# Two tiles of scores in flight in both attentions, and inversion blocks of one request beside the diagonal of the other

## The chip, the cores and the metric

One core of a Trainium2 chip runs the whole kernel. The metric is the device time of one execution in microseconds (us): 2386.69 is the median of three runs (2381.04 to 2390.11). The engines are TensorE (PE, with its weight loads PEld), VectorE (DVE), ScalarE (ACT), GpSimd (POOL) and SyncE (SP, which here issues nearly all DMAs).

## The reference

One encoder layer for two requests of 2048 tokens with 1024 features and shared weights. One projection feeds four mixing groups; their gated outputs are concatenated and projected back.

```python
def encoder_layer(x, mem, ...):
    hx = rms_norm(x, pre_g)
    a_u, a_z, b_qkv, b_z, b_gates, c_qkv, c_z, d_q, d_z = jnp.split(hx @ w_in, IN_SPLITS, axis=-1)
    y_a = fourier_mix(a_u, w_fnet) * jax.nn.silu(a_z)
    y_b = gdn_branch(b_qkv, b_gates, conv_w, a_log, dt_bias, gdn_g) * jax.nn.silu(b_z)
    cq, ck, cv = (t.reshape(b, l, N_HEADS_G, HEAD_DIM) for t in jnp.split(c_qkv, 3, axis=-1))
    y_c = neighbourhood_attn(cq, ck, cv, rpb) * jax.nn.silu(c_z)
    y_d = memory_attn(d_q, rms_norm(mem, mem_g), w_mem_kv) * jax.nn.silu(d_z)
    out = jnp.concatenate([y_a, y_b, y_c, y_d], axis=-1) @ w_out
    return x + rms_norm(out, post_g)
```

The gated DeltaNet group (GDN, `gdn_branch`) solves, for each chunk of 64 tokens, a unit lower triangular system `eye + l_mat`, in both directions of time, and then carries a state from chunk to chunk. Neighbourhood attention (NA) lets each token of a 32 x 64 grid see a window of 8 rows by 16 columns. Memory attention lets each token see 256 memory tokens of its request.

## The kernel before

Every matrix product is done in split fp16: the high and low half of each operand, three matmuls (`mm3`, L502: high by high, high by low, low by high). The program is written stage by stage in `build` (L1692). Each stage runs under a priority (`band`, L202), and a scheduler merges the stages at build time into one list for each engine, which that engine works off in its order. So a line that is written earlier need not run earlier. Tiles are taken from pools: a tile with `bufs` of n is n buffers in turn, and the n+1st waits for the last reader of the first. Pools lie on two stacks, left and right, and a pool in memory that another has left waits for that one's last users, stores included. PSUM banks are shared by tag in the same way.

The stages, as they follow in time:

- The GEMM passes: `pj` tiles on PE, evacuated to `st` tiles, stored to DRAM. `pass_z` and `pass_b` go on as fillers beside all that follows, up to 2000 us.
- `gdn_sub` (L1027), on the right stack, once for each request r. Each 64 x 64 triangle is inverted as two diagonal blocks of 32 and one block between. The diagonal: 31 steps on POOL (tile `pr`) and on DVE (PSUM tile `ppr`, tag `as`), each a product (L1064) and a sum (L1066). Then the results are split in halves (ACT L1079 and L1087, DVE L1080 and L1088) and stored to DRAM as `T` and `TO` (L1081, L1082, L1089); the parts go through `ol`, `lo`, `A` and `pr`. The blocks between: four tiles a request (d = 0, 1 and q = 0, 1), each with loads `ob`, a copy to `lb`, products `px` (tag `ga` for q = 0, `as` for q = 1), a split to `zb`, products `pz`, a split to `z`, and stores to `T`. Before the change request 0 is done in full, pool `psub0` and then `pblk0`, and request 1 then opens `psub1`.
- The GDN chain (`gdn_chain`, L1194): 32 steps, products `pc` and `pw`, loads of `T` by `cT`.
- Memory attention (`mem_attn`, L1458), on the left stack: 32 tiles, scores `pms`, softmax, transpose by DMA `mPT`, values `pmo`, output `pmy`. Its `na_setup` builds NA's bias table.
- NA (`na_attn`, L1551): 64 tiles. `scores`: products `pns` on PE, bias and maximum on DVE (`nS`), exponential on ACT, split into one of four padded tiles `np` (ACT L1640, DVE L1641), and a DMA transpose to `nPT` (L1643, two buffers). `values`: products `pno` with the loaded `nv`, evacuated by ACT to `nya` (L1669), stored as `yc` (L1671). As the code is written, the scores of tile i + 1 stand ahead of the values of tile i.
- The output projection (`pass_o`, L680, products `po`), 365 us. Its pool opens when the left stack is free, after NA.

Of the kernel before, what the change touches and what calls it, by code (L numbers as in the profile page):

```python
# [8 lines left out]
F32 = mybir.dt.float32  # L9
# [143 lines left out]
class Kern:  # L153
# [873 lines left out]
    def gdn_sub(self, r, side):  # L1027


        nc, D = self.nc, self.D  # L1030
        H = (slice(0, 32), slice(32, 64))
        row = lambda t, sl: t[:, sl].unsqueeze(1).to_broadcast([P, 32, 32])
        with self.tc.tile_pool(name=f"psub{r}", bufs=1, side=side) as pp:
            tl = lambda shape, dt, nme, b=1: pp.tile(shape, dt, name=self.nm(nme), tag=nme, bufs=b)
            Lu, nb, be, lp, T = {}, {}, {}, {}, {}
            zero = tl([P, 64], F16, "zero")
            nc.gpsimd.memset(zero, 0.0)
            for d in range(2):
                Lu[d] = D[f"L{r}_{d}"].rearrange("n h (q s) c -> (n h q) s c", q=2)
                self.dt([P, 64, 2, 2, 32], F16, f"T{r}_{d}")  # L1040
                self.dt([P, 32, 3, 2, 32], F16, f"TO{r}_{d}")
                nb[d], be[d] = tl([P, 64], F32, f"nbu{d}"), tl([P, 64], F32, f"beu{d}")
                nc.sync.dma_start(nb[d], D[f"nbd{r}"][d].rearrange("n h (q c) -> (n h q) c", q=2))
                nc.sync.dma_start(be[d], D[f"bed{r}"][d].rearrange("n h (q c) -> (n h q) c", q=2))

                lp[d] = tl([P, 2, 32, 32], F32, f"A{d}")
                for b in range(2):
                    nc.sync.dma_start(lp[d][:, b], Lu[d][:, H[b], H[b]])
                    self.gmul(lp[d][:, b], lp[d][:, b], row(nb[d], H[b]))
                T[d] = tl([P, 2, 32, 32], F32, f"T{d}")  # L1050
                nc.gpsimd.memset(T[d], 0.0)
                nc.gpsimd.memset(T[d].rearrange("p b i j -> p b (i j)")[:, :, 0:1024:33], 1.0)
            pr = tl([P, 2, 2, 256], F32, "pr")
            pq = self.pgd.tile([P, 2, 256], F32, name=self.nm("ppr"), tag="as")

            for k0 in range(31):
                for d in range(2):
                    k = k0 if d == 0 else 31 - k0
                    js, is_ = (slice(k + 1, 32), slice(0, k + 1)) if d == 0 else (slice(0, k), slice(k, 32))
                    nj, ni = js.stop - js.start, is_.stop - is_.start  # L1060
                    pv = [t.rearrange("p (j i) -> p j i", j=nj) for t in (pr[:, d, 0, 0:nj * ni], pq[:, d, 0:nj * ni])]
                    for b in range(2):
                        eng = nc.vector if b == 1 else nc.gpsimd
                        eng.tensor_tensor(out=pv[b], in0=lp[d][:, b, k, js].unsqueeze(2).to_broadcast([P, nj, ni]),  # L1064
                                          in1=T[d][:, b, k, is_].unsqueeze(1).to_broadcast([P, nj, ni]), op=ALU.mult)
                        eng.tensor_tensor(out=T[d][:, b, js, is_], in0=T[d][:, b, js, is_], in1=pv[b], op=ALU.add)  # L1066

            lo = [tl([P, 32, 32], F32, f"lo{d}") for d in range(2)]
            for d in range(2):
                nc.sync.dma_start(lo[d], Lu[d][:, H[d], H[1 - d]])  # L1070
                self.gmul(lo[d], lo[d], row(nb[d], H[1 - d]))
            for d in range(2):
                f, g = d, 1 - d
                TD = D[f"T{r}_{d}"]
                self.gmul(T[d][:, f], T[d][:, f], row(be[d], H[f]))
                ob = tl([P, 32, 2, 2, 32], F16, f"A{d}")
                ol = tl([P, 32, 2, 32], F16, "ol")
                for t, src in ((ob[:, :, 0], T[d][:, f]), (ob[:, :, 1], T[d][:, g].rearrange("p i j -> p j i")), (ol, lo[d])):
                    nc.scalar.activation(t[:, :, 0], src, AF.Copy)  # L1079
                    nc.vector.tensor_tensor(out=t[:, :, 1], in0=src, in1=t[:, :, 0], op=ALU.subtract)  # L1080
                nc.sync.dma_start(D[f"TO{r}_{d}"][:, :, 2].rearrange("p s l c -> p s (l c)"), ol.rearrange("p s l c -> p s (l c)"))  # L1081
                nc.sync.dma_start(D[f"TO{r}_{d}"][:, :, 0:2].rearrange("p s k l c -> p s (k l c)"), ob.rearrange("p s k l c -> p s (k l c)"))  # L1082
                self.gmul(T[d][:, g], T[d][:, g], row(be[d], H[g]))
                for b in (f, g):
                    t16 = tl([P, 32, 2, 32], F16, f"lo{d}" if b == f else ("pr", "ol")[d])
                    src = T[d][:, b].rearrange("p i j -> p j i")
                    nc.scalar.activation(t16[:, :, 0], src, AF.Copy)  # L1087
                    nc.vector.tensor_tensor(out=t16[:, :, 1], in0=src, in1=t16[:, :, 0], op=ALU.subtract)  # L1088
                    nc.sync.dma_start(TD[:, H[b], b].rearrange("p s l c -> p s (l c)"), t16.rearrange("p s l c -> p s (l c)"))  # L1089
                nc.sync.dma_start(TD[:, H[g], f].rearrange("p s l c -> p s (l c)"), zero.unsqueeze(1).to_broadcast([P, 32, 64]))  # L1090
        with self.tc.tile_pool(name=f"pblk{r}", bufs=1, side=side) as pp:
            tl = lambda shape, dt, nme, b=1: pp.tile(shape, dt, name=self.nm(nme), tag=nme, bufs=b)
            lbs = self.bds(pp, "lb", [P, 16, 2, 4, 32], F16, 2, nc.vector)
            zbs = self.bds(pp, "zb", [P, 16, 2, 4, 32], F16, 2)
            Q = [slice(32 * u, 32 * u + 32) for u in range(4)]
            fl = lambda t, i, l: t[:, i, l].rearrange("p a b -> p (a b)")
            for d in range(2):
                f, g = d, 1 - d
                for q in range(2):
                    ob = tl([P, 16, 3, 2, 32], F16, "ob", 2)  # L1100
                    z16 = tl([P, 16, 2, 32], F16, "z16", 2)
                    us = [slice(64 * q + u, 64 * q + 64, 4) for u in range(4)]
                    for u in range(4):
                        nc.sync.dma_start(ob[Q[u]].rearrange("s g k l c -> s g (k l c)"), D[f"TO{r}_{d}"][us[u]].rearrange("g s k l c -> s g (k l c)"))
                    lb, zb = lbs[q], zbs[q]
                    for u in range(4):
                        nc.vector.tensor_copy(lb[Q[u], :, :, u], ob[Q[u], :, 2])
                    px = self.pgd.tile([P, 16, 32], F32, name=self.nm("px"), tag=("ga", "as")[q])
                    for i in range(16):
                        self.mm3(px[:, i], fl(lb, i, 0), fl(lb, i, 1), ob[:, i, 0, 0], ob[:, i, 0, 1])  # L1110
                    for u in range(4):
# [647 lines left out]
```

## Time and profile before

| | |
|---|---|
| median of three runs | 2386.69 us |
| profiled execution, its own time | 2394.09 us |
| its span in the trace | 2392.2 us |
| mean granted clock of PE | 0.934 of full speed |
| busy share of PE, DVE, ACT, POOL | 82%, 75%, 48%, 43% |
| memory attention, first to last scores | 1127 to 1474 us |
| chain of GDN, first to last `pc` | 1326 to 1966 us |
| NA, first scores to last values | 1537 to 1993 us |
| from there to the first `po` | 1993 to 2027 us |
| output projection | 2027 to 2392 us |

The profile is one execution. A busy share is a mean over stages with different limits; each stage is read by itself, and there the question is which engine is idle and what ended its idle time. Matmuls are pipelined, so the step from one start to the next says more than the length of one.

### The profile page before, as it was taken

The numbers are of one execution on the slowest core, as the hardware profiler recorded it, in microseconds if no ns is written. First come the engines' busy times: TensorE is split into PE (matmuls) and PEld (weight loads), VectorE is DVE, ScalarE is ACT, GpSimd is POOL, SyncE is SP. The second block draws the span as 40 slices with busy tenths as digits, with TensorE's granted clock in tenths as the row PEclk, the third lists the DMA queues.
The fourth block names the chain that finished last, engine by engine and source line by source line (L and its number), as shares of the span: only waits on it lengthen the run. The fifth ranks groups of instructions, "written<-read, shape, count | busy, mean of one in ns | idle before, by whom it ended". The sixth has DMA issues, their size and how long they took to land.

```text
span 2392.2 us, 59873 instructions
## 1 busy us (share of the span) xinstructions
PE 1966.7 (82%) x23715; PEld 1685.4 (70%) x23715; DVE 1803.1 (75%) x4484; ACT 1158.4 (48%) x2562; POOL 1027.3 (43%) x1149
## 2 busy tenths in 40 slices
PE   0777787877557888898979999888888885999998
PEld 0566676666446777787758788877777774888887
DVE  3469978879999869968986687677787884665663
ACT  1446555444365322331675677476666674232332
POOL 1217655545477778219650433223343424323320
PEclk9898899999778999999989999999999997999999
DMA  9899999999756694879899999799999997545532
GB/s 91 192 226 208 223 244 224 239 203 253 199 125 181 201 187 141 177 161 211 193 209 194 236 229 240 211 220 215 211 222 231 204 216 225 175 182 209 202 144 106
DMA packets 827483, 476.06 MB, mean 199 GB/s; under 512 B 556865, under 2 KB 789953, under 8 KB 818753
## 3 DMA queue, kind: packets, MB, share of 16 engines
q1 hardware_dynamic: 802624, 438.67, 80.2%
q10 hardware_dynamic: 24576, 33.56, 4.7%
q8 instruction: 186, 3.05, 0.6%
q14 instruction: 97, 0.79, 0.1%
HBM read 243.38 MB, written 163.73 MB: 170 GB/s over the span
## 4 chain that ended last, share of the span: by engine, by line
PE 32%; DVE 27%; DMA 24%; SPq 5%; issue 5%; POOL 3%; ACT 3%; ACTq 0%; DVEq 0%; POOLq 0%
PE po L505 4%; PE po L504 4%; PE po L506 4%; PE pj L490 3%; PE pj L489 3%; PE pj L488 3%; DVE pcv L897 3%; DVE ppr L1064 2%; DMA nPT<-np__2868_27905 2%; DMA nPT<-np__2869_27907 2%; DMA xT<-xh 2%; DMA rec<-km 2%; DMA w<-in_w_in_dram 2%; DVE ty L239 2%; DMA nPT<-np__2871_27911 2%
## 5 line engine op out<-in xcount | busy, mean ns | idle before, releaser
L488 PE MATMUL pj<-xT,w 128*128 128x256 f16 x2592 | 729.8, 282 | 107.9 <-DMA xT<-xh 25.7
L490 PE MATMUL pj<-xT,w 128*128 128x256 f16 x2592 | 729.2, 281 | 9.7 <-POOL w L425 9.7
L489 PE MATMUL pj<-xT,w 128*128 128x256 f16 x2592 | 729.4, 281 | 0.0
L488 PEld LDWEIGHTS <-w 128*128 128x128 f16 x2592 | 261.1, 101 | 102.9 <-issue 36.1
L489 PEld LDWEIGHTS <-w 128*128 128x128 f16 x2592 | 261.2, 101 | 91.9 <-issue 54.3
L490 PEld LDWEIGHTS <-w 128*128 128x128 f16 x2592 | 261.5, 101 | 58.6 <-POOL w L425 11.5
L506 PE MATMUL po<-w,oy 128*128 128x256 f16 x1024 | 280.0, 274 | 2.1 <-DVE oy L720 2.1
L504 PE MATMUL po<-w,oy 128*128 128x256 f16 x1024 | 280.4, 274 | 0.7 <-DVE oo L771 0.7
L505 PE MATMUL po<-w,oy 128*128 128x256 f16 x1024 | 280.5, 274 | 0.0
L897 DVE SCALAR_TENSOR_TENSOR pcv<-craw,cws,pcv 128x256 f32<-128x256 f32 x384 | 176.3, 480 | 17.1 <-ACT pcv L895 14.8
L230 POOL TENSOR_TENSOR oy<-oy,oz 128x512 f32<-128x512 f32 x60 | 99.7, 1689 | 192.8 <-ACT oy L705 180.4
L769 ACT ACTIVATE oj<-po,wsc_o 128x256 f32<-128x256 f32 x128 | 59.5, 469 | 247.9 <-PE po L506 247.9
L1170 POOL COPY bk<-rA 64x512 f16<-64x512 f16 x124 | 87.9, 709 | 209.2 <-PE pw L506 148.0
L498 PE MATMUL pj<-w,xT 128*128 128x272 f16 (+1 forms) x512 | 147.5, 288 | 28.6 <-DVE st L213 17.2
L425 POOL TENSOR_TENSOR w<-wt,w 128x512 f16<-128x512 f32 (+1 forms) x70 | 86.2, 1240 | 151.6 <-ACT w L423 151.4
L499 PE MATMUL pj<-w,xT 128*128 128x272 f16 (+1 forms) x512 | 147.9, 289 | 0.9 <-POOL w L425 0.9
L500 PE MATMUL pj<-w,xT 128*128 128x272 f16 (+1 forms) x512 | 147.6, 288 | 0.0
L227 POOL TENSOR_TENSOR km<-kt,km 128x256 f16<-128x256 f32 x128 | 88.4, 711 | 65.7 <-ACT km L1016 59.6
L504 PE MATMUL pno<-nPT,nv 128*128 128x64 f16 x704 | 77.2, 199 | 46.7 <-DMA nPT<-np__2868_27905 13.0
L506 PEld LDWEIGHTS <-oy 128*128 128x128 f16 x1024 | 100.5, 98 | 14.4 <-DVE oy L720 2.6
L505 PEld LDWEIGHTS <-oy 128*128 128x128 f16 x1024 | 100.6, 98 | 13.2 <-issue 1.1
L504 PEld LDWEIGHTS <-oy 128*128 128x128 f16 x1024 | 100.5, 98 | 12.0
(441 smaller groups left out, 6005.4 us busy)
## 6 DMA issues: line engine op xcount, KB each, us to landing
xT<-xTd SPq DMA_DIRECT2D x32, 1024.0 KB
rec<-km SPq DMA_DIRECT2D x32, 768.0 KB
rA<-rec SPq DMA_DIRECT2D x64, 384.0 KB
xTd<-xT SPq DMA_DIRECT2D x16, 1024.0 KB
sz<-st ACTq DMA_DIRECT2D x64, 256.0 KB
oz<-sz SPq DMA_DIRECT2D x16, 1024.0 KB
out_dram<-oo SPq DMA_DIRECT2D x32, 512.0 KB
craw<-braw SPq DMA_DIRECT2D x48, 260.0 KB
```

The source lines that it names most:

```text
L227: self.nc.gpsimd.tensor_tensor(out=out, in0=a, in1=b, op=ALU.subtract)
L230: self.nc.gpsimd.tensor_tensor(out=out, in0=a, in1=b, op=ALU.mult)
L488: nc.tensor.matmul(ps, whi, xhi, start=(kt == 0), stop=False)
L489: nc.tensor.matmul(ps, whi, xlo, start=False, stop=False)
L490: nc.tensor.matmul(ps, wlo, xhi, start=False, stop=(kt == KT - 1))
L498: nc.tensor.matmul(ps, xhi, whi, start=(kt == 0), stop=False)
L499: nc.tensor.matmul(ps, xhi, wlo, start=False, stop=False)
L500: nc.tensor.matmul(ps, xlo, whi, start=False, stop=(kt == KT - 1))
L504: nc.tensor.matmul(ps, whi, xhi, start=start, stop=False)
L505: nc.tensor.matmul(ps, whi, xlo, start=False, stop=False)
L506: nc.tensor.matmul(ps, wlo, xhi, start=False, stop=stop)
L897: nc.vector.scalar_tensor_tensor(out=pcv[:, f], in0=raw[:, f, t:t + CB], scalar=w[:, t:t + 1], in1=pcv[:, f], op0=ALU.mult, op1=ALU.add)
```

## The change

In both attentions a list `ahead` holds the scores of two tiles; the scores of tile i + 2 are written ahead of the values of tile i. `nPT` gets a third buffer, and the loads of `nv` are called one position later, which leaves them where they were against the values. `na_setup` comes between the first two tiles of scores.

`gdn_sub` is called once. Its body is cut in two, `gdn_diag` (the diagonal, the splits and the stores; text as before but for `ol`) and `gdn_between` (the blocks between). Request 1's diagonal is opened after request 0's, and request 0's blocks inside it. To make room, the tile `ol` is dropped: `ol` and two of the four `t16` of each request now take turns in the single tile `pr`, which the diagonal steps on POOL use too; `lb`, `zb` and `z16` go from two buffers to one.

```diff
-    def gdn_sub(self, r, side):
+    def gdn_sub(self, side):
+        with self.tc.tile_pool(name="psub0", bufs=1, side=side) as pp:
+            self.gdn_diag(0, pp)
+        with self.tc.tile_pool(name="psub1", bufs=1, side=side) as pp:
+            self.gdn_diag(1, pp)
+            with self.tc.tile_pool(name="pblk0", bufs=1, side=side) as pb:
+                self.gdn_between(0, pb)
+        with self.tc.tile_pool(name="pblk1", bufs=1, side=side) as pb:
+            self.gdn_between(1, pb)
...
-                ol = tl([P, 32, 2, 32], F16, "ol")
+            ol = tl([P, 32, 2, 32], F16, "pr")
...
-                    t16 = tl([P, 32, 2, 32], F16, f"lo{d}" if b == f else ("pr", "ol")[d])
+                t16 = tl([P, 32, 2, 32], F16, f"lo{d}" if b == f else "pr")
...
-            lbs = self.bds(pp, "lb", [P, 16, 2, 4, 32], F16, 2, nc.vector)
-            zbs = self.bds(pp, "zb", [P, 16, 2, 4, 32], F16, 2)
+        lbs = self.bds(pp, "lb", [P, 16, 2, 4, 32], F16, 1, nc.vector)
+        zbs = self.bds(pp, "zb", [P, 16, 2, 4, 32], F16, 1)
...
-                    z16 = tl([P, 16, 2, 32], F16, "z16", 2)
+                z16 = tl([P, 16, 2, 32], F16, "z16")
...
-                    lb, zb = lbs[q], zbs[q]
+                lb, zb = lbs[0], zbs[0]
...
-            nxt = scores(*todo[0])
+            ahead = [scores(*todo[0])]
             self.na_setup(lambda: T([P, 2, 4, 256], F16, "mP16", 3).rearrange("p l h m -> p (l h m)").bitcast(F32))
+            ahead.append(scores(*todo[1]))
             for j, ri in enumerate(todo):
-                cur = nxt
-                if j + 1 < len(todo):
-                    nxt = scores(*todo[j + 1])
-                values(*ri, *cur)
+                if j + 2 < len(todo):
+                    ahead.append(scores(*todo[j + 2]))
+                values(*ri, *ahead.pop(0))
...
-                PT = T([P, 2, 2, 3, P], F16, "nPT", 2)
+                PT = T([P, 2, 2, 3, P], F16, "nPT", 3)
...
-            nxt = scores(*todo[0])
+            ahead = [scores(*ap) for ap in todo[:2]]
             for i, ap in enumerate(todo):
-                cur = nxt
-                if i + 1 < len(todo):
-                    nxt = scores(*todo[i + 1])
-                values(*ap, *cur)
+                if i + 2 < len(todo):
+                    ahead.append(scores(*todo[i + 2]))
+                values(*ap, *ahead.pop(0))
...
-                self.gdn_sub(0, "right")
-                self.gdn_sub(1, "right")
+                self.gdn_sub("right")
```

What the scheduler makes of it, at three places. First DVE, at request 0's blocks between. Before, the splits of the first two `px` tiles (`px_17080`, q = 0, and `px_17202`, q = 1) alternate, between FNet's steps and GEMM evacuations:

```order
L1337 TENSOR_TENSOR R_25512<-Z_25511 128x128
L213 SCALAR_TENSOR_TENSOR zh_25462<-R_25512,zh_25462 128x2048
L1113 TENSOR_TENSOR zb_17066<-px_17080,zb_17066 32x16x32
L1113 TENSOR_TENSOR zb_17068<-px_17202,zb_17068 32x16x32
L213 SCALAR_TENSOR_TENSOR st_7823<-pj_7774,st_7823 64x2x256
L1113 TENSOR_TENSOR zb_17066<-px_17080,zb_17066 32x16x32
L1113 TENSOR_TENSOR zb_17068<-px_17202,zb_17068 32x16x32
L213 SCALAR_TENSOR_TENSOR st_7823<-pj_7774,st_7823 64x2x256
```

After the change the second tile (`px_17529`, q = 1) is split right behind the last steps of request 1's diagonal, whose products are `ppr_17093`:

```order
L1075 TENSOR_TENSOR T_1718_17075<-T_1718_17075,ppr_17093 128x31
L1073 TENSOR_TENSOR ppr_17093<-A_1721_17084,T_1722_17089 128x31
L1075 TENSOR_TENSOR T_1722_17089<-T_1722_17089,ppr_17093 128x31
L614 CAST st_8535<-st_8536 128x2x256
L1119 COPY lb_17393<-ob_17641 32x32x32 x4
L1125 TENSOR_TENSOR zb_17395<-px_17529,zb_17395 32x16x32 x2
```

So the second `px`, and the third and fourth behind it, moved past all of request 1's diagonal; the first did not.

Second SP, where memory attention's loads are issued (`mks`, `mkl`, `mvb`, `mq`). Before, they stand behind request 1's store of `ol` only:

```order
L1081 DMA TO_1_17579<-ol_17871 4096x1x64
L478 DMA xT_8595<-xTd_6_3133 128x4096
L626 DMA cv_7280<-st_8372 128x2x512
L1474 DMA mks_25923<-mk_2261 128x1024
L1474 DMA mkl_25924<-ml_2263 64x1024
L1474 DMA mvb_25925<-mv_2317 128x1024
L1478 DMA mq_25929<-dq_5523 128x4x256
```

After the change:

```order
L478 DMA xT_9472<-xTd_1_214 128x4096
L1133 DMA T_1_16746<-z_1750_17764 32x16x64 x4
L1098 DMA T_1_17078<-pr_17385 128x32x64
L1486 DMA mks_25915<-mk_2261 128x1024
L1486 DMA mkl_25916<-ml_2263 64x1024
L1486 DMA mvb_25917<-mv_2317 128x1024
L1490 DMA mq_25921<-dq_5523 128x4x256
```

They moved behind the last store of request 1's diagonal (`T` from `pr_17385`) and behind request 0's last block store, 33 rows further down.

Third SP at the end of NA. Before, the last four transposes stand among weight loads (`w`) and stores of the chain's output (`yb`):

```order
L378 DMA w_12532<-in_w_out_dram 64x256 x4
L1644 DMA_TRANSPOSE nPT_32294<-np__2868_27905 128x12x128
L1671 DMA yc_3079<-nya_32088 256x1x256
L1644 DMA_TRANSPOSE nPT_32366<-np__2869_27907 128x12x128
L1300 DMA yb_7_3077<-osq_24952 128x256
L1644 DMA_TRANSPOSE nPT_32423<-np__2870_27909 128x12x128
L1300 DMA yb_7_3088<-osq_24955 128x256
L1300 DMA yb_0_3070<-osq_24958 128x256
L1644 DMA_TRANSPOSE nPT_32482<-np__2871_27911 128x12x128
```

After the change the last eight follow each other with only stores of NA's own output between them:

```order
L1655 DMA_TRANSPOSE nPT_31963<-np__2864_27897 128x12x128
L1655 DMA_TRANSPOSE nPT_32035<-np__2865_27899 128x12x128
L1682 DMA yc_3079<-nya_31823 256x1x256
L1655 DMA_TRANSPOSE nPT_32109<-np__2866_27901 128x12x128
L1655 DMA_TRANSPOSE nPT_32178<-np__2867_27903 128x12x128
L1655 DMA_TRANSPOSE nPT_32249<-np__2864_27897 128x12x128
L1655 DMA_TRANSPOSE nPT_32317<-np__2865_27899 128x12x128
L1682 DMA yc_3079<-nya_32111 256x1x256
L1655 DMA_TRANSPOSE nPT_32389<-np__2866_27901 128x12x128
L1655 DMA_TRANSPOSE nPT_32446<-np__2867_27903 128x12x128
L1682 DMA yc_3079<-nya_32391 256x1x256
```

The weight loads and the chain's stores moved ahead of NA's last tiles.

## Rows read from the trace of the kernel before

**Rows 1.** The page's fourth part: shares of the chain that ended last.

```profile
PE 32%; DVE 27%; DMA 24%; SPq 5%; issue 5%; POOL 3%; ACT 3%; ACTq 0%; DVEq 0%; POOLq 0%
```

**Rows 2.** Stretches: length, busy us of PE, PEld, DVE, ACT, POOL; clock; DMA share; GB/s.

```profile
1420.00:1535.00 115.00, 113.43 (x1870) 100.25 (x1871) 83.95 (x153) 66.69 (x123) 38.19 (x48) 1.00 0.95 233
1535.00:1650.00 115.00, 93.35 (x1757) 83.33 (x1755) 81.43 (x260) 73.64 (x161) 29.43 (x39) 0.90 0.88 205
1650.00:1760.00 110.00, 91.62 (x1795) 81.19 (x1794) 89.06 (x277) 72.98 (x169) 37.82 (x49) 0.94 1.04 220
1760.00:1870.00 110.00, 93.18 (x1732) 83.89 (x1728) 87.05 (x278) 74.19 (x165) 41.48 (x54) 0.94 1.06 228
1870.00:1990.00 120.00, 103.48 (x1974) 91.36 (x1973) 96.25 (x340) 85.03 (x208) 35.72 (x45) 0.99 1.02 211
1990.00:2027.00 37.00, 14.82 (x145) 12.15 (x143) 12.49 (x35) 18.59 (x36) 16.28 (x15) 0.69 0.79 262
```

**Rows 3.** Waits of PE, 1536 to 2030: who <- for what: total us, times, longest.

```profile
PE pno L504 <- DMA nPT<-np__2868_27905: 13.0, 5, 3.7
...
PE pno L504 <- DMA nPT<-np__2871_27911: 12.2, 7, 3.6
PE pno L504 <- DMA nPT<-np__2869_27907: 10.9, 8, 3.6
PE pno L504 <- DMA nPT<-np__2870_27909: 10.3, 3, 4.0
PE pc L1138 <- DVE S L1244: 9.0, 6, 3.1
```

**Rows 4.** DMA queues, 1536 to 1990: packets, MB, share of sixteen engines.

```profile
q1 hardware_dynamic: 193029, 89.27, 93.3%
```

**Rows 5.** Steps on PE: start, us, instruction; then the tile pns from 1536 to 1993.

```profile
1700.30 0.19 PE L506 MATMUL pno<-nPT,nv 128*128 128x64 f16 x1
...
1700.33 0.27 PE L489 MATMUL pj<-xT,w 128*128 128x256 f16 x1
...
1700.44 0.27 PE L490 MATMUL pj<-xT,w 128*128 128x256 f16 x1
...
1536.00:1993.00 457.00, 64.10 (x960) 45.45 (x128) 0.94 1.00 216
```

**Rows 6.** Inversions on POOL and DVE (time, us, instruction); last, memory attention's scores on PE.

```profile
952.44 3.33 POOL L230 TENSOR_TENSOR T<-T,beu 128x1024 f32<-128x1024 f32 x1
...
992.34 7.04 POOL L783 MEMSET zb<- 128x4096 f16 x2 [15.10 <-DMA cv<-st]
...
1062.27 0.15 POOL L1037 MEMSET zero<- 128x64 f16 x1 [37.24 <-DMA T<-z]
...
979.35 1.92 DVE L1088 TENSOR_TENSOR ol<-T,ol 128x1024 f16<-128x1024 f32 x1
...
1075.19 0.27 DVE L1064 TENSOR_TENSOR ppr<-A,T 128x31 f32<-128x31 f32 x1 [2.87 <-POOL A L230]
...
1183.98 0.20 DVE L1064 TENSOR_TENSOR ppr<-A,T 128x31 f32<-128x31 f32 x1
...
L1486 PE MATMUL pms<-mks,mq x128: 269/282/421, 1127.4 to 1474.1; 128*128 128x256 f16 x128
```

**Rows 7.** The longest wait of PE in 1063 to 1536.

```profile
PE pmy L1518 <- DVE ty L360: 8.1, 1, 8.1
```

**Rows 8.** Tiles pns, pno, pc on PE: count, ns, first and last start, forms.

```profile
L506 PE MATMUL pns<-nkr,nqb x320: 189/246/422, 1536.8 to 1970.9; 128*64 128x184 f16 x48, 128*64 128x253 f16 x48, 128*64 128x176 f16 x16, 128*64 128x128 f16 x13
...
L504 PE MATMUL pno<-nPT,nv x704: 189/193/257, 1563.5 to 1992.9; 128*128 128x64 f16 x176
...
L1138 PE MATMUL pc<-v,b x504: 193/193/242, 1337.0 to 1965.5; 128*128 128x64 f16 x168
```

**Rows 9.** The tile nS, 1536 to 1993: busy us on DVE and on ACT.

```profile
1536.00:1993.00 457.00, 104.65 (x256) 129.40 (x384) 0.94 1.00 216
```

**Rows 10.** The chain in order of time, 1990 to 2030: start, us, what.

```profile
1997.15 5.44 DMA yc<-nya
```

More of the change, by code (lines that the diff above doesn't have):

```diff
@@ new lines, in gdn_diag @@
+        tl = lambda shape, dt, nme, b=1: pp.tile(shape, dt, name=self.nm(nme), tag=nme, bufs=b)
+        Lu, nb, be, lp, T = {}, {}, {}, {}, {}
+        zero = tl([P, 64], F16, "zero")
+        nc.gpsimd.memset(zero, 0.0)
+        for d in range(2):
+            Lu[d] = D[f"L{r}_{d}"].rearrange("n h (q s) c -> (n h q) s c", q=2)
+            self.dt([P, 64, 2, 2, 32], F16, f"T{r}_{d}")
+            self.dt([P, 32, 3, 2, 32], F16, f"TO{r}_{d}")
+            nb[d], be[d] = tl([P, 64], F32, f"nbu{d}"), tl([P, 64], F32, f"beu{d}")
+            nc.sync.dma_start(nb[d], D[f"nbd{r}"][d].rearrange("n h (q c) -> (n h q) c", q=2))
+            nc.sync.dma_start(be[d], D[f"bed{r}"][d].rearrange("n h (q c) -> (n h q) c", q=2))
+            lp[d] = tl([P, 2, 32, 32], F32, f"A{d}")
+            for b in range(2):
+                nc.sync.dma_start(lp[d][:, b], Lu[d][:, H[b], H[b]])
+                self.gmul(lp[d][:, b], lp[d][:, b], row(nb[d], H[b]))
+            T[d] = tl([P, 2, 32, 32], F32, f"T{d}")
+            nc.gpsimd.memset(T[d], 0.0)
+            nc.gpsimd.memset(T[d].rearrange("p b i j -> p b (i j)")[:, :, 0:1024:33], 1.0)
@@ new lines, in gdn_diag @@
+        pr = tl([P, 2, 2, 256], F32, "pr")
+        pq = self.pgd.tile([P, 2, 256], F32, name=self.nm("ppr"), tag="as")
+        for k0 in range(31):
+            for d in range(2):
+                k = k0 if d == 0 else 31 - k0
+                js, is_ = (slice(k + 1, 32), slice(0, k + 1)) if d == 0 else (slice(0, k), slice(k, 32))
+                nj, ni = js.stop - js.start, is_.stop - is_.start
+                pv = [t.rearrange("p (j i) -> p j i", j=nj) for t in (pr[:, d, 0, 0:nj * ni], pq[:, d, 0:nj * ni])]
+                for b in range(2):
+                    eng = nc.vector if b == 1 else nc.gpsimd
+                    eng.tensor_tensor(out=pv[b], in0=lp[d][:, b, k, js].unsqueeze(2).to_broadcast([P, nj, ni]),
+                                      in1=T[d][:, b, k, is_].unsqueeze(1).to_broadcast([P, nj, ni]), op=ALU.mult)
+                    eng.tensor_tensor(out=T[d][:, b, js, is_], in0=T[d][:, b, js, is_], in1=pv[b], op=ALU.add)
@@ L1595, in scores @@
                         loadk(r, a + 2)
-                if p == 3 and nxt[0] < 2:
-                    loadv(*nxt, 0)
+                if p == 2:
+                    loadv(r, a, 2)
                 qv = qt[r, a].rearrange("p h l (b q) -> p (h l) b q", q=32)
```

134 lines of the change are left out of this document (53 added, 81 removed).

## Prediction

> **What bounds the kernel now.** I read the chain that ended last first [rows 1]: PE has only a third of it, DVE and the DMA engines the rest, so no one engine's work decides. The stage table [rows 2] then says where PE stands still. In the last stretch of memory attention PE is busy 113.4 of 115 us. In the four stretches of neighbourhood attention (NA) it is busy 93.35 + 91.62 + 93.18 + 103.48 = 381.6 of 455 us, so 73 us are idle, at a granted clock of 0.90 to 0.99; then come 37 us of changeover with 14.8 us of work. The waits of PE in NA [rows 3] name the idle time: `pno`, the values, waits 13.0 + 12.2 + 10.9 + 10.3 = 46.4 us in 23 waits for the transposed scores `nPT` to land, and the GDN chain `pc` waits 9.0 us, and more in smaller items, for its own state. The clock costs something beside: busy time at 0.90, 0.94, 0.94 and 0.99 would be shorter by 9.3 + 5.5 + 5.6 + 1.0 = 21 us at full clock. The DMA engines are as full as they get there (shares 0.88 to 1.06 in rows 2; 93.3% of sixteen engines' time goes to one queue's packets [rows 4]). The output projection waits for the end of NA, since its pool opens in the memory that NA leaves. So the end moves with NA's end, and that is PE's list up to there plus PE's idle time.
>
> **What the change does, step by step.** The list of PE has the same instructions; so the total of work is unchanged, and only what stands before NA's last values, and how long PE idles, counts. Steps per matmul [rows 5]: 0.11 us for `pj`, 0.03 us for the 64-column ones (`pc`, `pw`, `pno`), 64.10 us / 960 = 0.07 us for `pns`.
>
> (a) NA starts later. Memory attention's pool now waits for the last store of request 1's diagonal blocks (second fence of the change), and in PE's list 264 `pj`, 312 `pc` and 60 `pw` more stand ahead of NA's first score: 264 x 0.11 + 372 x 0.03 = 40 us. This is no loss by itself, for these leave NA's stretch; it decides who is left at the end, in (e).
>
> (b) The inversions. Three of request 0's four block tiles come behind request 1's diagonal, not beside it: `px` of every second tile uses the PSUM bank that the diagonal's `ppr` holds (first fence). `px_17529` stands behind 5831 `pj` matmuls; before, PE had run 5810 when memory attention began at 1127.4 [rows 6], so it can be there at about 1122 (three pairs of `px` and `pz`, 288 short matmuls, some 8 us, are no longer ahead). When is the diagonal done? Its start waits for request 0's stores, which now share the tile `pr`: one turn takes at most the 13 us from the split at 979.35 to 992.34, where POOL's memset has all of that pool's stores behind it (another load is named as its releaser). Four turns after POOL's last product before them, 955.8, make 1008; with other work between on DVE I allow up to 1035. Before, the first product was at 1075.19, 13 us after the pool had opened at 1062.27, and the last began at 1183.98 [rows 6]: 109 us, some of it other work on DVE, memory attention's above all, which is gone. So the first product comes at 1021 to 1048, and with 100 to 109 us the end falls at 1121 to 1157: PE loses 0 to 35 us, and I take +12. The tiles `lb` and `zb` with one buffer instead of two cost at most a part of the same wait. Request 1's blocks stand at the same `pj` count as before (6488 against 6501), so the chain's start stays.
>
> (c) `pmy` waited 8.1 us for DVE in the crowded stretch [rows 7]; memory attention has left it: -8 to 0, I take -4.
>
> (d) NA's waits. The code's second tile of scores is not new to PE: before, its list already starts 5.4 further tiles of scores (mean) between a tile's scores and its values, after 4.0. New is the third `nPT`, so that a transpose waits for the values of three tiles back, not two. All of 46.4 and the clock's 21 could go: -67. Nothing goes if the latency takes over: by the list, half of the value tiles stand 32 us of PE work behind their scores before and 21 us after, and the way from scores to values took 22 us where nothing else was left to do (last score 1970.9, last values 1992.9) and 26 for the first pair (1536.8 to 1563.5) [rows 8]. 22 to 26 us of latency against 21 us of work leave no lead over, and with the DMA engines full a wait for `nPT` comes back under another cause. I take about half of the ceiling: -32.
>
> (e) The tail. In the list before, 155 `pj`, 240 `pno` and 22 `pns` stand between the chain's last `pc` and NA's end, 17 + 7 + 2 = 26 us of work, and it took 1965.5 to 1992.9 [rows 8], 27 us. After the change 93 `pj`, 456 `pno` and 108 `pns` stand there, and behind the last `pj` still 312 `pno` and 72 `pns` (SP's last transposes stand with little between them, third fence): 9 tiles of scores and 14 of values with little to fill PE, 10 + 14 + 8 = 32 us of work. Beside the chain, 64 tiles of scores took 434 us (1536.8 to 1970.9), 6.8 us a tile. Alone they can't be faster than ACT, whose work on `nS` is 129.4 / 64 = 2.0 us a tile [rows 9], and with its work on the padded tiles and the values some 3 by my estimate. With 22 us for the last one: 9 x 3 + 22 = 49 to 9 x 6.8 + 22 = 83; I take 4 us a tile, 58. Idle time is then 58 - 32 = 26 (17 to 51) against 1 before, and I take +26, with a little for the half clock that an idle PE gets (0.69 in 1990 to 2027).
>
> (f) 60 `pj` move from behind NA's last values to ahead of them: +6.6. They lay beside the store of NA's last tile (1997.15, 5.44 us [rows 10]), which the loads of the output projection stand behind, so nothing comes back there. With fewer loads about, the changeover may be shorter by 0 to 5; I take -2. The output projection stays.
>
> Sum: 12 - 4 - 32 + 26 + 7 - 2 = +7 us. On the profiled run's own 2394.1 us that is 2401; this run lies 7.4 us over the median of the runs shown, so 2394 on the scale of the median. All terms at their ends would give 2387 - 8 - 67 + 17 + 7 - 5 = 2331 and 2387 + 35 + 51 + 7 = 2480, but they won't come together.
>
> **The rivals.**
> *Faster: the buffers were all.* The 23 waits are alike, up to 4.0 us each, and stand all along the stage [rows 3], which speaks for it; if PE then gets the full clock too, (d) is -58. With the tail at its lower end, +17, (b) 6 and the rest: 6 - 6 - 58 + 17 + 7 - 4 = -38, 2349. The Trainium skill ("Perfetto Trace Analysis", Optimization Strategy) names this reading: a gap that repeats on the engine that should be full can mean that there is no room for the next tile. By that rule alone the gain would be this rival's. Against it stand the full DMA engines and the shorter lead of scores over values.
> *Slower: NA is left over.* If NA alone goes no faster than beside the chain, 6.8 us a tile, since transposes, softmax and stores follow each other whatever PE does, (e) is +51. With (d) at -20 and (b) at 12: 12 - 4 - 20 + 51 + 7 - 2 = +44, 2431. With (d) at -20 the sum without (e) is -7, so it is over +12 as soon as (e) is over 19, which 3.2 us a tile already make; with (d) at -32 it takes 31, or 4.5 us a tile. For it: the last eight tiles' values stand only 4 to 10 us of work behind their scores. Against: ACT and DVE are half empty.
> *It doesn't do what it says.* One of four block tiles runs beside the diagonal, scores had been ahead anyway, and the DMA engines are full, so a third buffer only lengthens their queue: each term is near 0, about 2387.
>
> **How the numbers follow.** Forecast 0.41 (2378 to 2412), faster rival 0.27, slower rival 0.22, no effect 0.10. A measurement here tells about 0.5% from no change, 12 us. Of the forecast's 0.41, 0.25 lie within 12 us of 2387 and 0.16 above. Faster: 0.27 and 0.02 of the last case, 0.29; within: 0.25 + 0.08 = 0.33; slower: 0.16 + 0.22 = 0.38. About a tenth lies beyond each rival's middle, so the range is 2344 to 2434; the forecast's own is 2378 to 2412.
>
> **What the profile after would show.** (a) NA's first `pns` at 1570 to 1595; (b) a wait of `px` or `pz` for DVE near 1125 to 1155; (d) PE's waits for `nPT` down from 46 to 15 or 25 us, and the clock of NA's stretches up; (e) a stretch of 50 to 65 us at the end of NA with PE busy for about half of it. I am wrong if waits for `nPT` stay (the DMA engines or the softmax set them), or vanish with a tail under 45 us, or if NA doesn't start later.

## The result and the profile after

The changed kernel takes 2417.05 us in the median of four runs (2404.43 to 2424.2), the kernel before 2388.4 us in four beside them. The ratio is 1.0101, 95% interval 1.0066 to 1.0137: about 24 us slower, by 16 to 33. (The two medians lie 29 us apart; the ratio is used throughout.) The profiled execution took 2404.43 us (span 2402.6), the fastest of its four.

One thing has to be known ahead of any comparison. Up to FNet's first `pdf` PE runs the same 5406 matmuls in the same order in all kernels here, and yet that point comes at other times. In the tile view (count, ns, first and last start) of the kernel before, and then of the changed one, for several tiles:

```profile
L504 PE MATMUL pdf<-tab,zh x64: 269/273/418, 836.8 to 1064.8; 128*128 128x256 f16 x64
```

```profile
L504 PE MATMUL pdf<-tab,zh x64: 272/273/417, 825.3 to 1071.9; 128*128 128x256 f16 x64
...
L1498 PE MATMUL pms<-mks,mq x128: 269/283/396, 1202.1 to 1520.1; 128*128 128x256 f16 x128
...
L506 PE MATMUL pns<-nkr,nqb x320: 189/246/415, 1569.9 to 1996.4; 128*64 128x184 f16 x48, 128*64 128x253 f16 x48, 128*64 128x176 f16 x16, 128*64 128x128 f16 x13
...
L1150 PE MATMUL pc<-v,b x504: 193/193/242, 1312.7 to 1950.8; 128*128 128x64 f16 x168
...
L504 PE MATMUL pno<-nPT,nv x704: 189/193/242, 1597.3 to 2011.0; 128*128 128x64 f16 x176
...
L504 PE MATMUL po<-w,oy x1024: 272/273/421, 2039.7 to 2393.1; 128*128 128x256 f16 x171
```

836.8 against 825.3: the profile after has 11.5 us of luck in it ahead of everything that was changed. Counted from the first `pdf`, memory attention's first scores come at 377 us (before 291), NA's first at 744 (700), the chain's last product at 1126 (1129), NA's last values at 1186 (1156), the first `po` at 1214 (1190). That is the 24 us of the timed ratio. All times "from `pdf`" below are such differences.

The stages (length, busy us of PE, PEld, DVE, ACT, POOL, clock, DMA share, GB/s), which answer to [rows 2]:

```profile
1420.00:1535.00 115.00, 114.01 (x1828) 96.22 (x1827) 89.33 (x176) 81.98 (x169) 34.03 (x43) 0.99 0.99 230
...
1650.00:1760.00 110.00, 90.13 (x1756) 79.89 (x1755) 92.47 (x288) 70.93 (x156) 40.20 (x53) 0.94 0.99 221
1760.00:1870.00 110.00, 91.00 (x1673) 81.90 (x1672) 83.60 (x264) 70.96 (x164) 36.98 (x49) 0.90 1.04 220
1870.00:1990.00 120.00, 92.59 (x1747) 83.15 (x1743) 98.08 (x356) 89.36 (x218) 38.10 (x44) 0.91 0.90 201
1990.00:2040.00 50.00, 18.53 (x285) 16.53 (x286) 14.14 (x53) 17.69 (x47) 6.85 (x6) 0.57 0.62 184
```

Memory attention's last stretch is as full as before. In 1870 to 1990 PE is busy 92.6 us where it was 103.5, and 50 us follow with 18.5 us of work at a clock of 0.57: the end of NA and the changeover. PE's waits from 1536 to 2050, which answer to [rows 3]:

```profile
PE pno L504 <- DMA nPT<-np__2864_27897: 26.3, 8, 5.9
...
PE pno L504 <- DMA nPT<-np__2866_27901: 12.5, 4, 5.6
PE pno L504 <- DMA nPT<-np__2867_27903: 11.8, 5, 7.6
PE pno L504 <- DMA nPT<-np__2865_27899: 10.5, 7, 4.0
```

The waits of the values for `nPT` have not fallen from 46.4 us; they are 26.3 + 12.5 + 11.8 + 10.5 = 61.1.

### The profile page after: what moved, and what is told of

Its sections match the earlier page's. It is cut to its first block, busy times and chain, and to the rows that moved or that the text cites. A ratio compares the mean times of both kernels' runs of the same rounds, so it can differ in the third digit from the quotient of the medians.

```text
span 2402.6 us, 59852 instructions
## 1 busy us (share of the span) xinstructions
PE 1967.8 (82%) x23715; PEld 1691.1 (70%) x23715; DVE 1799.5 (75%) x4482; ACT 1158.6 (48%) x2562; POOL 1011.8 (42%) x1147
## 5 line engine op out<-in xcount | busy, mean ns | idle before, releaser
L498 PE MATMUL pj<-w,xT 128*128 128x272 f16 (+1 forms) x512 | 151.2, 296 | 37.9 <-DVE st L213 20.8
L499 PE MATMUL pj<-w,xT 128*128 128x272 f16 (+1 forms) x512 | 151.2, 295 | 0.9 <-POOL w L425 0.9
L500 PE MATMUL pj<-w,xT 128*128 128x272 f16 (+1 forms) x512 | 150.9, 295 | 0.0
L504 PE MATMUL pno<-nPT,nv 128*128 128x64 f16 x704 | 80.8, 203 | 62.8 <-DMA nPT<-np__2864_27897 26.3
L1189 ACT ACTIVATE b<-rA 64x1536 f16<-64x1536 f16 x64 | 92.3, 1474 | 38.6 <-PE pc L1150 26.5
L506 PEld LDWEIGHTS <-oy 128*128 128x128 f16 x1024 | 100.7, 98 | 13.1 <-DVE oy L720 1.3
L505 PEld LDWEIGHTS <-oy 128*128 128x128 f16 x1024 | 100.8, 98 | 12.2
```

The source lines that it names most:

```text
L498: nc.tensor.matmul(ps, xhi, whi, start=(kt == 0), stop=False)
L499: nc.tensor.matmul(ps, xhi, wlo, start=False, stop=False)
L500: nc.tensor.matmul(ps, xlo, whi, start=False, stop=(kt == KT - 1))
L504: nc.tensor.matmul(ps, whi, xhi, start=start, stop=False)
L505: nc.tensor.matmul(ps, whi, xlo, start=False, stop=False)
L506: nc.tensor.matmul(ps, wlo, xhi, start=False, stop=stop)
```

## The experiments

Each line of this table is one kernel: the ratio to the kernel before on the same chip with its interval, and, from its profile, five points in us from the first `pdf`. Between the first `pdf` and the first `po` PE has the same work in all of them, so the last column shows what PE lost in that one execution. One profile stands behind each row: against the timed ratio the last column is off by -7 to +16 us (after_ga: 10 us over before, where the ratio says 6 under), so it tells where time goes, and the ratio how much.

| kernel | ratio (95%) | memory first | NA first | chain last | NA last | `po` first |
|---|---|---|---|---|---|---|
| before | 1 | 291 | 700 | 1129 | 1156 | 1190 |
| the change | 1.0101 (1.0066 to 1.0137) | 377 | 744 | 1126 | 1186 | 1214 |
| gdn_only | 1.0110 (1.0076 to 1.0145) | 382 | 739 | 1141 | 1192 | 1220 |
| att_only | 0.9983 (0.9957 to 1.0008) | 293 | 695 | 1140 | 1154 | 1196 |
| na_only | 0.9973 (0.9943 to 1.0003) | 291 | 705 | 1138 | 1156 | 1195 |
| npt3 | 0.9997 (0.9969 to 1.0025) | 293 | 703 | 1144 | 1172 | 1204 |
| after_ga | 0.9973 (0.9946 to 1.0000) | 296 | 711 | 1128 | 1169 | 1200 |
| ga_old | 1.0057 (1.0031 to 1.0083) | 295 | 710 | 1153 | 1188 | 1220 |
| before_fill | 1.0144 (1.0123 to 1.0164) | 396 | 769 | 1121 | 1206 | 1235 |
| gdn_bufs | 1.0123 (1.0076 to 1.0169) | 286 | 689 | 1198 | 1182 | 1234 |
| after_zlate | 1.0104 (1.0062 to 1.0146) | 380 | 729 | 1105 | 1136 | 1208 |
| att_zlate | 1.0227 (1.0200 to 1.0255) | 290 | 675 | 1134 | 1124 | 1252 |
| half_t | 1.0119 (1.0073 to 1.0166) | 291 | 703 | 1146 | 1195 | 1222 |
| no_lo | 0.9977 (0.9955 to 0.9998) | 291 | 700 | 1118 | 1156 | 1195 |

A second table says where PE lost it: time less work in each stretch, in us. Work is counted from the matmuls in the trace at the steps of [rows 5] (0.11 us for 256 columns, in proportion for fewer, 0.067 us for `pns`); from the first `pdf` to the first `po` it is 918 us in every kernel.

| kernel | up to NA's first scores | on to the chain's last product | on to NA's last values | changeover | in all |
|---|---|---|---|---|---|
| before | 139 | 104 | 2 | 26 | 273 |
| the change | 144 | 94 | 30 | 28 | 297 |
| gdn_only | 145 | 101 | 30 | 26 | 302 |
| att_only | 147 | 111 | 3 | 18 | 279 |
| after_ga | 144 | 110 | 7 | 21 | 282 |
| ga_old | 151 | 127 | 5 | 19 | 302 |
| before_fill | 191 | 85 | 16 | 25 | 317 |
| after_zlate | 147 | 124 | 2 | 17 | 290 |

In the changed kernel the loss lies behind the chain's last product: 28 us more there, 10 less in the stretch before it.

### Which part costs: gdn_only and att_only

The first has the changed `gdn_sub` and the old attentions, the second the old `gdn_sub` and the changed attentions.

> Only the inversions are changed (gdn_diag and gdn_between, request 0's blocks inside request 1's diagonal, ol in pr, single lb, zb, z16); both attentions as before. Theory A (the loss comes from NA starting later and being left over at the end): the list puts NA's first scores 33 us of PE work later than before and leaves 21 us of NA's work, with little to fill, behind the chain's last product; NA ends 15 to 30 us later than before and the time is 2400 to 2420, about that of the whole change. Theory B (the loss comes from the attentions, whose scores lead their values by less): within 8 us of the kernel before.

> Only the attentions are changed (two tiles of scores in the list ahead, three nPT buffers, loadv one position later); the inversions as before. Theory A: NA starts no later than before (13 us of PE work earlier in the list), only 12 us of its work stand behind the chain's last product, GEMM fillers stand behind its end and cover the changeover: 2355 to 2380, faster than both. Theory B: the shorter lead of scores over values (median 23 us of PE work against 32) makes PE wait more for nPT: 2395 to 2415.

The inversions alone cost 1.1%, 26 us; the attentions alone are -0.2%, -4 us, an interval from -10 to +2. The sum, 22 us, is the change's own 24 within the noise, so nothing points to an effect of the two together. Theory A had the first one right (though NA ends 36 us later, not 15 to 30) and the second one wrong: the attentions don't slow the kernel, but they don't gain the 20 us either, and theory B's line for them isn't met. In the tile view of gdn_only the tail is the one of the changed kernel, 51 us from the chain's last product to NA's last values:

```profile
L506 PE MATMUL pns<-nkr,nqb x320: 189/246/422, 1571.6 to 2008.6; 128*64 128x253 f16 x50, 128*64 128x184 f16 x48, 128*64 128x176 f16 x15, 128*64 128x128 f16 x13
...
L1150 PE MATMUL pc<-v,b x504: 193/193/242, 1324.1 to 1972.3; 128*128 128x64 f16 x168
...
L504 PE MATMUL pno<-nPT,nv x704: 189/193/242, 1601.2 to 2023.5; 128*128 128x64 f16 x176
```

### Why the inversions cost: after_ga and before_fill

```diff
-                px = self.pgd.tile([P, 16, 32], F32, name=self.nm("px"), tag=("ga", "as")[q])
+                px = self.pgd.tile([P, 16, 32], F32, name=self.nm("px"), tag="ga")
```

> The changed kernel with all four px tiles of a request in the PSUM tag ga, so that none shares the bank of the diagonal's ppr; nothing else. In PE's list the second px of request 0 comes at 140 us of work behind the first pdf instead of 240, memory attention's first scores at 245 instead of 315 (where they stood before the change), NA's at 628 instead of 661, and the last GEMM tiles again behind NA's end. Theory A (the late px tiles hold the pool that memory attention waits for, so NA is late and left over): the loss goes, within 10 us of the kernel before. Theory B (the split itself costs, by its stores in turns through pr and by single buffers): 15 to 30 us over the kernel before, as the changed kernel.

First the chain of events in the changed kernel, from its timeline (start, us, engine, line, operation):

```profile
1016.26 0.15 POOL L1046 MEMSET zero<- 128x64 f16 x1 [0.41 <-DMA T<-pr]
...
1030.35 0.27 DVE L1073 TENSOR_TENSOR ppr<-A,T 128x31 f32<-128x31 f32 x1 [2.94 <-POOL A L230]
...
1112.38 0.19 DVE L1075 TENSOR_TENSOR T<-T,ppr 128x31 f32<-128x31 f32 x1
...
1112.62 0.18 PE L504 MATMUL px<-ob,lb 128*128 128x32 f16 x1
...
1186.90 2.68 SPq L1133 DMA_DIRECT2D T<-z  x4
1189.68 2.89 SPq L1098 DMA_DIRECT2D T<-pr  x1
1195.38 1.39 SPq L1486 DMA_DIRECT2D mks<-mk  x1
```

and SP's own wait at these loads in 1185 to 1200 (total us, times, longest):

```profile
SPq L1486 <- DMA T<-z: 2.7, 2, 2.2
```

Request 1's diagonal opens at 1016 and frees the PSUM bank with its last sum at 1112.38; PE starts the second `px` of request 0 0.24 us later. Three of the four block tiles that were to run beside the diagonal run behind it (the first, with `px` at 982.5, had run ahead of it); their last store is issued at 1186.90, and SP waits for that store (`T` from `z`) before it issues memory attention's loads. In after_ga, where nothing but the bank differs, the same loads in the timeline, and its tiles:

```profile
1142.15 0.58 SPq L1486 DMA_DIRECT2D mks<-mk  x1
```

```profile
L504 PE MATMUL pdf<-tab,zh x64: 269/273/421, 853.2 to 1111.1; 128*128 128x256 f16 x64
...
L1498 PE MATMUL pms<-mks,mq x128: 269/283/396, 1149.5 to 1505.0; 128*128 128x256 f16 x128
...
L504 PE MATMUL pno<-nPT,nv x704: 189/193/242, 1598.7 to 2022.1; 128*128 128x64 f16 x176
```

Memory attention starts 296 us from `pdf`, and in the timed ratio the 24 us are gone (-0.3%). In the second table the idle time behind the chain's last product falls from 30 to 7 us, while 16 come back in the stretch before it; this profile by itself shows 14 of the 24 us gone. In this list the loads `mks` stand behind request 0's last block store, but ahead of request 1's diagonal stores. So the pool that memory attention waits for is the one of request 0's blocks, held open by the PSUM bank, and not request 1's diagonal. Theory B falls for the changed order: after_ga has the same turns in `pr` and the same single buffers.

before_fill makes memory attention late by another way, in the old order:

```diff
             pr = tl([P, 2, 2, 256], F32, "pr")
+            if r == 1:
+                fill = tl([P, 13312], F16, "fill")
+                nc.gpsimd.memset(fill[:, 0:1], 0.0)
```

> The kernel before with an unused tile of 26 KB for each partition in request 1's psub pool, so that memory attention's pool does not fit beside it and opens only when it closes; the inversions' order is the old one. NA's first scores come 18 us of PE work later than before and 67 us of work stand behind the chain's last product, but 47 of them have GEMM tiles among them up to the end. Theory A1 (NA's late start costs by itself): 15 to 25 us slower. Theory A2 (only a tail without filler costs): within 8 us of before.

```profile
L504 PE MATMUL pdf<-tab,zh x64: 269/273/421, 847.8 to 1077.8; 128*128 128x256 f16 x64
...
L1489 PE MATMUL pms<-mks,mq x128: 269/283/421, 1243.9 to 1544.6; 128*128 128x256 f16 x128
...
L504 PE MATMUL pno<-nPT,nv x704: 189/193/242, 1632.9 to 2053.4; 128*128 128x64 f16 x176
```

Memory attention starts 105 us later than before, NA ends 50 us later, and the kernel is 1.4% slower, 34 us, though GEMM tiles stand in its list up to the end. That is more than A1's line had and far from A2's. But it is not the changed kernel's loss made another way. In the second table it loses 51 us more than before ahead of NA's first scores, where the changed kernel lost 5 more, and from there on 7 less. PE's longest wait in 1110 to 1244, just ahead of memory attention's first scores, is for a load of the GEMM passes:

```profile
PE pj L488 <- DMA xT<-xTd: 14.9, 1, 14.9
```

So the run shows that a pool that opens late costs in the old order too, but not that NA's late start by itself does. What it has of A2: with GEMM tiles in NA's end, NA's stretch has no more idle time than before (85 + 16 against 104 + 2). The cause of the change's loss rests on after_ga and on the timelines.

### Is it the bare tail: after_zlate and att_zlate

```diff
-                self.pass_z(0)
-                self.pass_z(1)
+            with self.band(2.5):
+                self.pass_z(0)
+                self.pass_z(1)
```

> The changed kernel with the gate projections (pass_z) at a priority behind both attentions, so that they fill in last: NA's values end at 918 us of work behind the first pdf instead of 972, and 55 us of GEMM tiles stand behind them. Theory A2 (the loss is PE idle in the tail and the changeover): the loss goes and the changeover is covered, 15 to 40 us faster than the changed kernel, at or under the kernel before. Rival (PE's idle time in NA is NA's own latency, and with fewer fillers among its tiles it grows by what the tail gives): no faster than the changed kernel.

> The kernel with both attentions changed and the old inversions, with the gate projections behind both attentions: NA's values end at 856 us of work instead of 949, and 117 us of GEMM tiles stand behind them. Theory A2: the changeover is covered and the end gains 20 to 30 us over the kernel before. Rival: the chain and NA alone leave PE idle longer, which the tiles at the end do not give back: 0 to 25 us slower than before.

```profile
L504 PE MATMUL pdf<-tab,zh x64: 269/273/421, 847.8 to 1097.2; 128*128 128x256 f16 x64
...
L506 PE MATMUL pns<-nkr,nqb x320: 189/246/415, 1576.7 to 1969.2; 128*64 128x184 f16 x48, 128*64 128x253 f16 x48, 128*64 128x176 f16 x18, 128*64 128x92 f16 x14
...
L504 PE MATMUL pno<-nPT,nv x704: 189/193/242, 1603.3 to 1983.9; 128*128 128x64 f16 x176
...
L490 PE MATMUL pj<-xT,w x2592: 269/273/421, 72.3 to 2046.1; 128*128 128x256 f16 x200
```

A2's forecast fails. In after_zlate NA ends at 1136 us from `pdf`, 20 us ahead of the kernel before, and PE has GEMM tiles to do in the changeover; it is as slow as the changed kernel. The idle time behind the chain is gone (30 to 2 us) and the changeover's is less (28 to 17), but the stretch before has 124 us of it instead of 94. From NA's first scores to its last values PE had 36 us less work (281 against 317) and took 34 us less time (407 against 441): the idle time in NA stayed and only moved forward. att_zlate moves more work behind NA and loses more, 54 us, which is over its rival's 0 to 25: 171 us idle from NA's first scores to its last values, against 114 in att_only. So moving `pass_z` costs by itself, and after_zlate can't say what the tail alone is worth. What both show is that fillers taken out of NA leave PE idle there.

### Inversions by themselves: ga_old and gdn_bufs

ga_old is after_ga with the old attentions; gdn_bufs is the kernel before with `ol` in `pr` and single `lb`, `zb` and `z16` in the old order.

> The changed inversions with all px tiles in the PSUM tag ga, attentions as before. In the list memory attention and NA start where they did before (245 and 619 us of work), the chain too. If running request 0's blocks beside request 1's diagonal is worth something once they don't delay memory attention: 5 to 20 us faster than before. If what the inversions save lies beside the GEMM work anyway: within 8 us of before, and equal to the run with ga and the changed attentions.

> The kernel before with what the change took from the inversions' buffers and nothing else: ol in turns with pr, one lb, zb and z16; old order of the requests, old attentions. If the turns and single buffers cost what the changed inversions cost: 15 to 30 us slower. If only the late memory and neighbourhood attention cost: NA's first scores stand 35 us of PE work earlier than before in this list, the chain's first product 25 us later, and the time is within 12 us of before.

Without the shared bank the inversions gain nothing with the old attentions: +0.6%, which neither of the two lines had. Nor is it much of an overlap: in after_ga request 0's four `px` start at 1012 to 1062, and request 1's diagonal has its first product at 1067. It does end 50 us earlier than before, counted from `pdf` (297 against 347), but the chain's first product comes only some 10 us earlier (479 against 489). gdn_bufs costs 1.2%, as its first line had it, but by another part: what comes late there is the chain. The tile view of gdn_bufs:

```profile
L504 PE MATMUL px<-ob,lb x128: 176/176/179, 1022.2 to 1315.4; 128*128 128x32 f16 x128
...
L1138 PE MATMUL pc<-v,b x504: 193/193/241, 1382.7 to 2034.1; 128*128 128x64 f16 x168
```

Its last `px` starts 480 us from `pdf` (before 448), and the chain ends at 1198 (1129). So single buffers and turns in `pr` cost as much in the old order. In the changed order they are not what costs, since the chain doesn't come late there (1126) and after_ga, which has them too, is no slower than before.

One thing limits the account of the bank. With the old attentions the same edit gives back only about half of the loss (gdn_only 1.0110, ga_old 1.0057), though memory attention and NA start in time (295 and 710) and the idle time behind the chain is gone (5 us); 23 us more than before are lost between NA's first scores and the chain's last product. Why after_ga and ga_old, which differ by the attentions alone, lie 0.8% apart when att_only and before lie 0.2% apart stays open: each edit makes the scheduler plan every list anew, and no run here holds a list fixed.

### Why the attentions gain nothing: npt3, na_only, half_t and no_lo

> The kernel before with a third nPT buffer and nothing else. If the buffer was what PE waited for: the 46 us of waits for nPT fall under 20 and the time to 2350 to 2370. If the scheduler gives the buffer's gain back by setting the values closer behind their scores (lead 22 us of PE work against 32 in the list): waits of 40 us or more stay, now with SP's transposes waiting for DVE's softmax instead of for PE, and the time is within 10 us of before.

> Only NA is changed (two tiles of scores, three nPT buffers); memory attention and the inversions as before. Theory A: NA's first scores stand where they stood, 15 us of NA's work behind the chain: 2365 to 2388. Theory B: lead 20 us of PE work against 32: 2395 to 2415, with PE's waits for nPT over 60 us. If it equals the run with both attentions changed, memory attention's part is worth nothing.

npt3 has the third `nPT` buffer and nothing else. PE's waits in NA stay, 15.2 + 15.2 + 14.6 + 9.0 = 54 us:

```profile
PE pno L504 <- DMA nPT<-np__2868_27905: 15.2, 5, 5.5
PE pno L504 <- DMA nPT<-np__2870_27909: 15.2, 5, 5.7
PE pno L504 <- DMA nPT<-np__2871_27911: 14.6, 7, 3.2
PE pno L504 <- DMA nPT<-np__2869_27907: 9.0, 9, 3.1
```

What changed is whom SP's transposes wait for. In the kernel before, the queue's waits at that line (total us, times, longest):

```profile
SPq L1644 <- PE pns L506: 19.9, 12, 4.2
SPq L1644 <- PE pno L506: 16.6, 9, 3.6
SPq L1644 <- PE pw L506: 14.6, 11, 2.7
SPq L1644 <- PE pc L1138: 12.4, 6, 3.6
...
SPq L1644 <- PE pj L490: 8.1, 5, 2.6
```

and in npt3, the four longest:

```profile
SPq L1644 <- DVE ty L1623: 11.6, 4, 3.7
SPq L1644 <- DVE S L1238: 11.4, 4, 5.0
SPq L1644 <- DVE ty L1625: 11.3, 4, 5.3
SPq L1644 <- DVE ty L1630: 8.6, 3, 4.9
```

Before, 72 us of their waits ended with PE and 10 with DVE; in npt3 it is 21 and 78. By the code a transpose needs PE only for the last readers of its `nPT`, so the third buffer did free it, and what it waits for now is DVE: three of the four lines above are NA's softmax, L1238 is the chain's. The values had moved up: half of them stand 23 us of PE work behind their scores, where it was 32. The run came out as its second line had it: the buffer's gain went into the shorter lead, and the wait came back one step further up. na_only has the short lead too (21 us) and the time of the kernel before (0.9973); its waits for `nPT` are 40.8 us, not the over 60 of its theory B. att_only lies as close (0.9983), so memory attention's two tiles add nothing that can be seen.

The two remaining runs ask what sets the pace of NA, 7 us a tile beside the chain.

```diff
-                nc.sync.dma_start(PT.rearrange(...), pads.rearrange(...), transpose=True)
+                for x in range(2):
+                    nc.sync.dma_start(PT[:, x, 0], pads[:, x, 0].rearrange("p r c -> p (r c)"), transpose=True)
...
-                            self.mm3(..., PT[:, 0, g, qs], PT[:, 1, g, qs], ...)
+                            self.mm3(..., PT[:, 0, g, qs], PT[:, 0, g, qs], ...)
```

> The kernel before with NA's transposes cut to the high half of the probabilities (two DMA transposes a tile, each of a quarter of the former blocks); the values use the high half in place of the low one too, so the output lacks the low half's part. Work of every engine, and the order up to NA, are as before. Theory D (NA's pace beside the chain, 7.1 us a tile, is set by the DMA engines, which are full there): NA takes 380 to 430 us instead of 456 and the end comes 20 to 50 us earlier. Theory S (it is set by the way through softmax on DVE and ACT and their queues): NA keeps 445 to 465 us, the time is within 10 us.

```profile
1650.00:1760.00 110.00, 92.13 (x1818) 81.55 (x1816) 90.12 (x278) 74.55 (x164) 39.46 (x51) 0.97 0.84 189
1760.00:1870.00 110.00, 87.65 (x1548) 78.53 (x1545) 78.48 (x244) 63.60 (x136) 38.80 (x50) 0.94 0.83 191
```

With half of the data transposed the DMA share is 0.83 to 0.84 in stretches where it was 1.04 to 1.06, and the waits for `nPT` don't fall (who waited, us, times):

```profile
  PE pno L504: 62.0, 27
```

NA took 491 us instead of 456, which neither line had. Theory D falls: full DMA engines were not what held the values. That it became slower has to do with two transposes to issue for a tile, or with the new lists; the run can't tell.

```diff
-                    nc.vector.scalar_tensor_tensor(out=lo, in0=Sv, scalar=sm[:, 3, x:x + 1], in1=hi, op0=ALU.mult, op1=ALU.subtract)
```

> The kernel before without the low half of the probabilities on DVE (128 instructions of about 0.5 us, 62 us of DVE in NA's stage); the low planes stay zero and are transposed all the same, so the output lacks that part. Theory D: NA's pace and the time stay within 10 us. Theory S: a tile gets 1 us of DVE work and a step of latency less, NA takes 400 to 430 us and the end comes 20 to 40 us earlier.

```profile
L506 PE MATMUL pns<-nkr,nqb x320: 189/246/422, 1531.6 to 1964.4; 128*64 128x253 f16 x48, 128*64 128x184 f16 x46, 128*64 128x176 f16 x16, 128*64 128x92 f16 x13
...
L504 PE MATMUL pno<-nPT,nv x704: 189/193/242, 1556.3 to 1986.9; 128*128 128x64 f16 x176
```

455 us, as before, with 62 us less work on DVE: theory S falls too, as far as it is a matter of DVE's work. What sets NA's pace is open. One reading is that the lists are planned to a model, so that whatever is made cheaper is turned into a shorter lead of the scores over their values. It fits npt3 and na_only, where the lead fell from 32 to 23 and 21 us; in half_t and no_lo it is still 29, so for them it explains little. It was only argued: a list that is kept while one cost changes would test it, and wasn't tried.

## Why the prediction was right or wrong, step by step

The forecast was 2394 us in 2344 to 2434, within 0.5% of before or slower. Measured is 2417, and 2387 x 1.0101 = 2411 on the scale of the median before: in the range, 17 us above the forecast, at the upper end of the forecast case. Some of that is luck: (b) was 12 us too dear and made up for half of what (d) promised too much. By its own sign the prediction was wrong about NA: it would be wrong "if waits for `nPT` stay", and they rose from 46 to 61 us.

- (a) Right in size: 40 us of work in front of NA, NA's first scores 44.5 us later from `pdf`. The reason was wrong in part. I named request 1's diagonal stores, because they stand right ahead of memory attention's loads in SP's list; SP's wait (`T` from `z`) and after_ga show that it is request 0's last block store, one row above.
- (b) The bank was seen, its price was not where I looked for it. I had +12 for PE waiting at the second `px`; PE lost no time there. Pool and first product came at 1016 and 1030, inside my bounds (one reading was off: POOL's last product before starts at 959.75, not 955.8, so the four turns make 1012), but the diagonal, with no memory attention on DVE beside it yet, took 82 us instead of 100 to 109. No `px` waited; one `pz` waited 2.1 us, for ACT. The bank's price was (a), through the pool.
- (c) -4 forecast; `pmy`'s 8.1 us of [rows 7] are gone, its longest sort of wait is 0.9.
- (d) is the step that failed: -32 forecast, -4 (-10 to +2) with the attentions alone. From NA's first scores to the chain's last product the second table has 94 us lost, against 104 before: 10 less. The bound "nothing goes if the latency takes over" was in the text, with the shorter lead as its reason, and is what npt3 fits; I took half of the ceiling from [rows 3] instead. But my figure for that latency doesn't hold: in the 22 us from the last score to the last values PE also ran 147 `pj`, some 16 us, and in the changed kernel, with none of them left, the same way took 14.6 us (1996.4 to 2011.0). The Trainium skill ("Perfetto Trace Analysis", Optimization Strategy) says that a repeated gap can mean missing room for the next tile; here room was what SP waited for, and giving it moved the wait (npt3, 0.9997).
- (e) Right for this list: 60.2 us from the chain's last product to NA's last values (1950.8 to 2011.0), 58 forecast, which is 4.2 us a tile, with 30 us idle where I had 26. As a remedy, filling the tail was not enough: after_zlate has no such idle time there, has it in NA instead and is as slow.
- (f) The changeover took 28.7 us instead of 34, -5; -2 forecast.

With the measured sizes, by the second table: +5 ahead of NA, -10 in it up to the chain's end, +28 of idle time in the tail, +1 for (f) (7 us of work gone from the changeover, 5 us of its time), together the 24 that the profiles differ by up to `po`.

Of the rivals, "NA is left over" came nearest in time: its point was 3.2 us a tile with (d) at -20, and the tail took 4.2. "It doesn't do what it says" had nearly the right fact, one block tile of four beside the diagonal (it ran ahead of it, and none beside), and the wrong conclusion, that this leaves everything as it was.

## What to carry to other kernels

An overlap that is written into the code has to be looked for in the engines' lists: here one shared PSUM bank kept three of four tiles from it and held the pool open that memory attention waited for, and the price came up at the end of NA, a stage further on. Where a scheduler plans the lists, a freed buffer may be spent on a shorter lead (here 32 to 23 us), so look after the edit whether the wait is gone or has only changed its releaser. Compare two profiles from the last point up to which the lists are the same, since what lies ahead of it moved here by half of the effect.

No version beat the kernel before beyond doubt: after_ga and na_only lie at -0.3%, with intervals that reach no change; no_lo, at -0.2% and just clear of it, leaves out part of the output.

## What the runs showed of the hardware

The identical start of the lists, up to the first `pdf`, took 825 to 837 us in ten profiles and 848 to 854 in the four that were run together on one chip (after_ga, before_fill, after_zlate, att_zlate). On that chip the kernel before had a median of 2416.9 us, against 2388.4, 2397.4 and 2398.0 in the three other sets. The first stage, which the change doesn't touch, was 19 us longer there in the mean (851 against 832), as much as the medians of the later sets differ by; the kernel before itself was not profiled on that chip.
